# Weight-stationary projections with 256-column matmuls alone and one 256-column accumulator

## The chip, the cores and the metric

One core of a Trainium2 chip runs the whole kernel. The metric is device time in microseconds (us); a lower time is better. TensorE (PE) does the matmuls and PEld is its loading of weights, VectorE is DVE, ScalarE is ACT, GpSimd is POOL, and SyncE (SP) issues most DMAs.

## What is computed

Two residual layers over 256 positions of width 2048, each with an RMS norm ahead, and a final RMS norm. Layer 0 projects the normed input to an SSD (state-space) head group and a gated position-mixing group and projects both back; layer 1 is differential attention with 16 heads. All of it is float32.

```python
def reference(x, norm_w, even_w_in, ..., odd_w_in, ..., odd_w_out, final_norm_w):
    h = x
    for layer in range(DEPTH):
        hn = rmsnorm(h, norm_w[layer])
        i = layer // 2
        if layer % 2 == 0:
            h = h + even_mixer(hn, even_w_in[i], ...)
        else:
            h = h + odd_mixer(hn, odd_w_in[i], ...)
    return rmsnorm(h, final_norm_w)
```

In `even_mixer`, `proj = h @ w_in` is split into the SSD's gate, its x, B and C (which pass a convolution of four taps), and u, v and a gate for the position mixing; the results are concatenated and multiplied by `w_out`. In `odd_mixer`, `proj = h @ w_in` is split into q, k, v and a gate, and the attended values are multiplied by `w_out`. These four weight matrices are nearly all of the work.

## The kernel before

Every float32 operand of a large product is split into a high part in float32r and the remainder (`split` for weights, L115; `put_split` for activations, L202), and a product is the sum of three: high x high, high x low and low x high. Activations lie transposed in tiles of [128, 16, 2, 256]: 16 blocks of the contraction, the high and the low part, 256 positions.

Weights come in tiles of 128 x 2048 floats (1 MB), by one DMA each from SP's queue (`fetch`, L122). ACT writes the high part `wh` (L118) and DVE the low part `wl` (L119), in two halves of 1024 columns, with three buffers for each of `raw`, `wh` and `wl`.

Two forms of projection follow. In the weight-stationary form (`t_accum` and `t_half`, L132 to L147) a tile holds 128 output features, and PE loads a 128 x 128 block of weights and streams activations past it. It is used for B, C and x of the SSD (`conv_block`, L328), u and zb of the gating stage (L489 to L499), q and k (`qk_block`, L577) and both output projections (`out_proj`, L519). In the token-major form (`tok_proj`, L159) the activations are the stationary operand and weights stream in 512 columns; it makes z, v and the gates and is the same in both kernels.

A half tile in the weight-stationary form is 8 matmuls of 512 columns, in which `wh` meets high and low activations side by side, and then 8 of 256 columns, in which `wl` meets the high part:

```python
pe.matmul(ps, lhsT=wh[:, i, :], rhs=x[:, k, :, :].rearrange("p a b -> p (a b)"),
          start=first and k == 0, stop=False)
...
pe.matmul(ps[:, 256:512], lhsT=wl[:, i, :], rhs=x[:, k, 0, :],
          start=False, stop=last and k == 15)
```

So the accumulator `ps` (one of four PSUM banks of 512 columns, `acc`, L149) ends with high x high in its first 256 columns and the sum of the two low products in the last 256. `t_sum` (L152) joins them: ACT copies the low half to `sm` (L154), DVE adds the high half to give `t` (L156). `out_proj` does the same with L541 to L543. The one exception is the last block of the second output projection (n = 15 of "o1", L525): it already has three 256-column matmuls for each block k, in the order `wl`, `wh`, `wh`, into one accumulator (L531).

The first two tiles, B0 and C0, are handled apart at the start (L225 to L262), interleaved with the projection for dt (L245). `token_rstd` (L181) makes the norm's factor for each position: a column sum `pc_n` on PE (L187), `ms_n` on DVE, `rt_n` on POOL, a broadcast `pb_n` on PE (L194), and the copy `rb0` on ACT (L199). DVE multiplies each projection by `rb0` (L335 for the SSD, into `xp`) or `rb1` (L583).

The order of the instructions is made by a scheduler in the framework, which lists every engine's instructions by a timeline of its own; an engine then runs its list in order, and waits on semaphores.

Of the kernel before, what the change touches and what calls it, by code (L numbers as in the profile page):

```python
# [9 lines left out]
F32 = mybir.dt.float32  # L10
F32R = mybir.dt.float32r
AF = mybir.ActivationFunctionType
ALU = mybir.AluOpType
# [4 lines left out]
P = 128  # L18
S = 256
# [53 lines left out]
def hybrid_trunk(ctx: ExitStack, tc: tile.TileContext, xT, cols, dskip, dtp, lnw, lnb, sgub, wsT,  # L73
                 wdt, w0, wo0, w1, wo1, outT):
    nc = tc.nc
    v, act, pe, pool = nc.vector, nc.scalar, nc.tensor, nc.gpsimd
# [50 lines left out]
    def halves(src, inner, nm):  # L127
        raw = fetch(src, nm).rearrange("p (a b) -> p a b", b=inner)
        n = 2048 // inner // 2
        return [split(raw[:, h * n:(h + 1) * n, :], [n, inner], f"{nm}_{h}") for h in range(2)]  # L130

    def t_half(ps, hv, x, half, first, last):  # L132
        wh, wl = hv
        for i in range(8):
            k = half * 8 + i
            pe.matmul(ps, lhsT=wh[:, i, :], rhs=x[:, k, :, :].rearrange("p a b -> p (a b)"),  # L136
                      start=first and k == 0, stop=False)
        for i in range(8):
            k = half * 8 + i
            pe.matmul(ps[:, 256:512], lhsT=wl[:, i, :], rhs=x[:, k, 0, :],  # L140
                      start=False, stop=last and k == 15)

    def t_accum(ps, src, x, first, last, nm):

# [3 lines left out]

    def acc(nm):  # L149
        return acc_p.tile([P, 512], F32, tag="acc", name=f"acc_{nm}")  # L150

    def t_sum(ps, nm):  # L152
        sm = ev.tile([P, S], F32, tag="sm", name=f"sm_{nm}")
        act.activation(sm, ps[:, 256:512], AF.Copy)  # L154
        t = ev.tile([P, S], F32, tag="t", name=f"t_{nm}")
        v.tensor_tensor(t, ps[:, 0:256], sm, op=ALU.add)  # L156
        return t

    def tok_proj(srcs, x, nm):  # L159
        ps = [acc(f"{nm}_{i}") for i in range(2)]  # L160
# [48 lines left out]
    with ExitStack() as l0:  # L209
# [116 lines left out]
        def conv_block(blk, nm):  # L326
            if nm in ("B0", "C0"):
                ps = first_ps["BC".index(nm[0])]  # L328
            else:
                ps = acc(nm)  # L330
                t_accum(ps, nxt(w0), xw, True, True, nm)
            t = t_sum(ps, nm)
            xp = sp.tile([P, S + 3], F32, tag="xp", name=f"xp_{nm}", bufs=3)
            pool.memset(xp[:, 0:3], 0.0)
            v.tensor_tensor(xp[:, 3:S + 3], t, rb0, op=ALU.mult)  # L335
            cv = sp.tile([P, S], F32, tag="cv", name=f"cv_{nm}")
            act.activation(cv, xp[:, 0:S], AF.Identity, scale=c1(C_CW + blk * 4), bias=c1(C_CB + blk))
            for k in range(1, 4):
                v.scalar_tensor_tensor(cv, xp[:, k:S + k], c1(C_CW + blk * 4 + k), cv,
                                       op0=ALU.mult, op1=ALU.add)  # L340
            return cv
# [105 lines left out]
    with ExitStack() as l0b:  # L447
# [19 lines left out]
        for j in range(16):  # L467
            n = f"j{j}"
            if j % 4 == 0:
                qd = j // 4  # L470
                qs = slice(qd * 512, (qd + 1) * 512)
                lw = gp_.tile([P, 512], F32, tag="lw", name=f"lw{qd}")
                lb = gp_.tile([P, 512], F32, tag="lb", name=f"lb{qd}")
                pool.dma_start(lw, lnw[qs].rearrange("(o a) -> o a", o=1).broadcast_to([P, 512]))
                pool.dma_start(lb, lnb[qs].rearrange("(o a) -> o a", o=1).broadcast_to([P, 512]))
                with tc.issue_after(last_split[1]):
                    for tb in range(2):
                        v.tensor_scalar(vt[:, tb, qs], vt[:, tb, qs], nmu[:, tb:tb + 1], vr[:, tb:tb + 1],
                                        op0=ALU.add, op1=ALU.mult)
                    for t, op in ((lw, ALU.mult), (lb, ALU.add)):  # L480
                        v.tensor_tensor(vt[:, :, qs], vt[:, :, qs],
                                        bc(t.rearrange("p (o a) -> p o a", o=1), [P, 2, 512]), op=op)
                ws_t = gp_.tile([P, 4, P], F32, tag="ws", name=f"ws_{n}")
                pool.dma_start(ws_t, wsT[:, j:j + 4, :])
                pool.affine_select(out=ws_t, in_=ws_t, compare_op=ALU.is_ge, fill=0.0, base=0,
                                   pattern=[[0, 4], [1, P]], channel_multiplier=-1)
                sb_t = gp_.tile([P, 4, P], F32, tag="sb", name=f"sb_{n}")
                pool.dma_start(sb_t, sgub[j:j + 4, :].rearrange("(o a) b -> o a b", o=1).broadcast_to([P, 4, P]))
            ps = acc(f"u{j}")  # L489
            t_accum(ps, nxt(w0), xw, True, True, f"u{j}")  # L490
            t = t_sum(ps, f"u{j}")
            u = gp_.tile([P, S], F32, tag="u", name=f"u_{n}", bufs=3)
            v.tensor_tensor(u, t, rb0, op=ALU.mult)
            act.activation(u, u, AF.Gelu_apprx_tanh)
            ps = acc(f"zb{j}")
            t_accum(ps, nxt(w0), xw, True, True, f"zb{j}")
            t = t_sum(ps, f"zb{j}")
            zb = gp_.tile([P, S], F32, tag="zb", name=f"zb_{n}", bufs=3)
            v.tensor_tensor(zb, t, rb0, op=ALU.mult)  # L499
            act.activation(zb, zb, AF.Silu)  # L500
            pm = aux(f"pm_{n}")
            for c in range(2):
                pe.matmul(pm[:, c * P:(c + 1) * P], lhsT=vt[:, c, j * P:(j + 1) * P], rhs=ws_t[:, j % 4, :],
                          start=True, stop=True)
            mx = gp_.tile([P, 2, P], F32, tag="mx", name=f"mx_{n}")
            v.tensor_tensor(mx, pm[:, 0:S].rearrange("p (c t) -> p c t", t=P),
                            bc(sb_t[:, j % 4:j % 4 + 1, :], [P, 2, P]), op=ALU.add)
            mx = mx.rearrange("p c t -> p (c t)")
            v.tensor_tensor(mx, mx, u, op=ALU.mult)
            v.tensor_tensor(mx, mx, zb, op=ALU.mult)  # L510
            act.activation(yb[:, j, 0, :], mx, AF.Copy)
            v.tensor_tensor(yb[:, j, 1, :], mx, yb[:, j, 0, :].bitcast(F32), op=ALU.subtract)
# [6 lines left out]
    def out_proj(w, nm, after):  # L519


        pool.memset(sqa, 0.0)
        for n in range(16):
            ps = acc(f"{nm}_{n}")
            if n == 15 and nm == "o1":  # L525
                for half, x in enumerate((ya, yb)):
                    hv = halves(w[2 * n + half], P, f"{nm}_{n}{half}")
                    for k in range(16):
                        wh, wl = hv[k // 8][0][:, k % 8, :], hv[k // 8][1][:, k % 8, :]
                        for m, (lhsT, part) in enumerate(((wl, 0), (wh, 1), (wh, 0))):  # L530
                            pe.matmul(ps[:, 0:256], lhsT=lhsT, rhs=x[:, k, part, :], start=half + k + m == 0,  # L531
                                      stop=half == 1 and k == 15 and m == 2)
                v.tensor_tensor(res[:, n, :], ps[:, 0:256], res[:, n, :], op=ALU.add)
                sq = ev.tile([P, S], F32, tag="sqo", name=f"sq_{nm}_{n}")
                act.activation(sq, res[:, n, :], AF.Square)
                after(n)
                continue
            t_accum(ps, w[2 * n], ya, True, False, f"{nm}_{n}a")
            t_accum(ps, w[2 * n + 1], yb, False, True, f"{nm}_{n}b")
            sm = ev.tile([P, S], F32, tag="sm", name=f"sm_{nm}_{n}")  # L540
            act.activation(sm, ps[:, 256:512], AF.Copy)  # L541
            v.tensor_tensor(res[:, n, :], ps[:, 0:256], res[:, n, :], op=ALU.add)
            v.tensor_tensor(res[:, n, :], res[:, n, :], sm, op=ALU.add)  # L543
            sq = ev.tile([P, S], F32, tag="sqo", name=f"sq_{nm}_{n}")
            act.activation(sq, res[:, n, :], AF.Square)
            if n < 15:
                pool.tensor_tensor(sqa, sqa, sq, op=ALU.add)
            after(n)
        return [sqa, sq]
# [6 lines left out]
    with ExitStack() as l1:  # L556
# [20 lines left out]
        def qk_block(tag, c0, nm):  # L577

            ps = acc(nm)
            t_accum(ps, nxt(w1), xw, True, True, nm)  # L580
            t = t_sum(ps, nm)
            o = ap.tile([P, S], F32, tag=tag, name=nm)
            v.tensor_tensor(o, t, rb1, op=ALU.mult)  # L583
            hl = ap.tile([P, 2, S - c0], F32R, tag=tag + "hl", name=f"{nm}_hl")
            act.activation(hl[:, 0, :], o[:, c0:S], AF.Copy)
            v.tensor_tensor(hl[:, 1, :], o[:, c0:S], hl[:, 0, :].bitcast(F32), op=ALU.subtract)
            return o, hl
# [166 lines left out]
```

## Time and profile before

| | |
|---|---|
| Median of 3 runs | 1724.22 us (1722.86 to 1724.52) |
| The profiled execution: its own time | 1724.63 us |
| The profiled execution: span on the core | 1722.9 us |
| PE busy | 1702.2 us (99%), 9232 matmuls |
| PEld busy | 1460.7 us (85%) |
| DVE busy | 1126.6 us (65%) |
| ACT busy | 990.1 us (57%) |
| POOL busy | 106.0 us (6%) |
| DMA | 318.68 MB, 185 GB/s on average |

Busy time is the union of an engine's instructions. Matmuls overlap: each one's start is measured and its end is modelled, so the distance from one start to the next is what a matmul costs in a stream. In a row of the timeline the first number is the start of the first of xN instructions of one kind, and the second the time that they cover; the step within a run is the distance to the start of the next row, divided by N.

### The profile page before, as it was taken

The numbers are of one execution on the slowest core, as the hardware profiler recorded it, in microseconds if no ns is written. First come the engines' busy times: TensorE is split into PE (matmuls) and PEld (weight loads), VectorE is DVE, ScalarE is ACT, GpSimd is POOL, SyncE is SP. The second block draws the span as 40 slices with busy tenths as digits, with TensorE's granted clock in tenths as the row PEclk, the third lists the DMA queues.
The fourth block names the chain that finished last, engine by engine and source line by source line (L and its number), as shares of the span: only waits on it lengthen the run. The fifth ranks groups of instructions, "written<-read, shape, count | busy, mean of one in ns | idle before, by whom it ended". The sixth has DMA issues, their size and how long they took to land.

```text
span 1722.9 us, 23833 instructions
## 1 busy us (share of the span) xinstructions
PE 1702.2 (99%) x9232; PEld 1460.7 (85%) x9232; DVE 1126.6 (65%) x1704; ACT 990.1 (57%) x1521; POOL 106.0 (6%) x159
## 2 busy tenths in 40 slices
PE   7999999999999999999999999999999999999997
PEld 6888888888888888888888888888888888888886
DVE  6897869545777665556566666757576666655554
ACT  6776776546777744445455555555554555555443
POOL 3200000100000011110000000000000000001110
PEclk9999999999999999999999999999999999999998
DMA  7555444655655565555455455455545555445552
GB/s 254 207 175 195 172 159 171 218 198 191 216 205 173 194 236 184 193 194 172 172 188 177 171 173 191 173 173 173 184 169 184 174 180 184 171 172 196 195 191 104
DMA packets 46290, 318.68 MB, mean 185 GB/s; under 512 B 5280, under 2 KB 5584, under 8 KB 9440
## 3 DMA queue, kind: packets, MB, share of 16 engines
q1 hardware_dynamic: 44400, 310.30, 51.3%
q0 software_dynamic: 1344, 4.24, 0.9%
q10 hardware_dynamic: 432, 2.61, 0.4%
q8 instruction: 72, 1.18, 0.3%
q14 instruction: 42, 0.34, 0.1%
HBM read 315.00 MB, written 2.13 MB: 184 GB/s over the span
## 4 chain that ended last, share of the span: by engine, by line
PE 95%; DVE 1%; ACT 1%; issue 1%; POOL 1%; DMA 0%; SPq 0%; DVEq 0%; POOLq 0%; ACTq 0%
PE acc_o L136 13%; PE acc_q L136 7%; PE acc_k L136 7%; PE acc_o L140 7%; PE acc_v L170 5%; PE acc_v L172 5%; PE acc_v L171 5%; PE acc_q L140 3%; PE acc_g L172 3%; PE acc_k L140 3%; PE acc_g L170 3%; PE acc_g L171 3%; PE acc_u L136 3%; PE acc_zb L136 3%; PE acc_x L136 3%; PE acc_u L140 2%
## 5 line engine op out<-in xcount | busy, mean ns | idle before, releaser
L118 ACT ACTIVATE wh_v<-raw_v 128x1024 fp32r<-128x1024 f32 x96 | 101.8, 1060 | 109.1 <-PE acc_v L172 88.7
L119 DVE TENSOR_TENSOR wl_v<-raw_v,wh_v 128x1024 fp32r<-128x1024 f32 x96 | 117.6, 1225 | 68.3 <-ACT wh_v L118 67.4
L171 PE MATMUL acc_v<-wl_v,xw 128*128 128x512 f32 x384 | 152.2, 396 | 0.0
L172 PE MATMUL acc_v<-wh_v,xw 128*128 128x512 f32 x384 | 151.6, 395 | 0.0
L170 PE MATMUL acc_v<-wh_v,xw 128*128 128x512 f32 x384 | 142.8, 397 | 0.0
L136 PE MATMUL acc_q<-xw,wh_q 128*128 128x512 f32 x512 | 131.8, 393 | 0.0
L119 DVE TENSOR_TENSOR wl_g<-raw_g,wh_g 128x1024 fp32r<-128x1024 f32 x64 | 78.4, 1226 | 80.6 <-ACT wh_g L118 80.6
L136 PE MATMUL acc_k<-xw,wh_k 128*128 128x512 f32 x512 | 130.8, 395 | 0.0
L118 ACT ACTIVATE wh_g<-raw_g 128x1024 fp32r<-128x1024 f32 x64 | 67.9, 1060 | 80.5 <-PE acc_g L172 53.5
L119 DVE TENSOR_TENSOR wl_q<-raw_q,wh_q 128x1024 fp32r<-128x1024 f32 x64 | 77.8, 1225 | 52.0 <-ACT wh_q L118 46.5
L118 ACT ACTIVATE wh_k<-raw_k 128x1024 fp32r<-128x1024 f32 x64 | 67.8, 1059 | 70.2 <-PE acc_q L136 30.2
L118 ACT ACTIVATE wh_q<-raw_q 128x1024 fp32r<-128x1024 f32 x64 | 67.8, 1059 | 68.3 <-PE acc_g L172 23.9
L136 PEld LDWEIGHTS acc_k<-xw,wh_k 128*128 128x128 f32 x512 | 91.6, 188 | 16.2
L136 PEld LDWEIGHTS acc_q<-xw,wh_q 128*128 128x128 f32 x512 | 90.5, 188 | 15.6
L172 PE MATMUL acc_g<-wh_g,xw 128*128 128x512 f32 x256 | 101.5, 397 | 0.0
L171 PE MATMUL acc_g<-wl_g,xw 128*128 128x512 f32 x256 | 101.0, 394 | 0.0
L119 DVE TENSOR_TENSOR wl_k<-raw_k,wh_k 128x1024 fp32r<-128x1024 f32 x64 | 78.3, 1224 | 26.8 <-ACT wh_k L118 26.7
L170 PE MATMUL acc_g<-wh_g,xw 128*128 128x512 f32 x256 | 92.2, 396 | 0.0
L170 PEld LDWEIGHTS acc_v<-wh_v,xw 128*128 128x128 f32 x384 | 72.0, 187 | 16.5
L172 PEld LDWEIGHTS acc_v<-wh_v,xw 128*128 128x128 f32 x384 | 72.0, 188 | 16.3
L171 PEld LDWEIGHTS acc_v<-wl_v,xw 128*128 128x128 f32 x384 | 72.0, 188 | 16.0
L140 PE MATMUL acc_q<-xw,wl_q 128*128 128x256 f32 x512 | 73.8, 281 | 0.0
(500 smaller groups left out, 4012.6 us busy)
## 6 DMA issues: line engine op xcount, KB each, us to landing
raw_v<-in_w_dram SPq DMA_DIRECT2D x48, 1024.0 KB, 4.8
raw_q<-in_w_dram SPq DMA_DIRECT2D x32, 1024.0 KB, 4.7
raw_k<-in_w_dram SPq DMA_DIRECT2D x32, 1024.0 KB, 4.8
raw_g<-in_w_dram SPq DMA_DIRECT2D x32, 1024.0 KB, 4.8
raw_x<-in_w_dram SPq DMA_DIRECT2D x16, 1024.0 KB, 4.8
raw_z<-in_w_dram SPq DMA_DIRECT2D x16, 1024.0 KB, 4.8
raw_u<-in_w_dram SPq DMA_DIRECT2D x16, 1024.0 KB, 4.8
raw_zb<-in_w_dram SPq DMA_DIRECT2D x16, 1024.0 KB, 4.8
```

Of the source, the lines that this page charges most:

```text
L118: last_split[0] = act.activation(wh, raw, AF.Copy).ins
L119: last_split[1] = v.tensor_tensor(wl, raw, wh.bitcast(F32), op=ALU.subtract).ins
L136: pe.matmul(ps, lhsT=wh[:, i, :], rhs=x[:, k, :, :].rearrange("p a b -> p (a b)"), start=first and k == 0, stop=False)
L140: pe.matmul(ps[:, 256:512], lhsT=wl[:, i, :], rhs=x[:, k, 0, :], start=False, stop=last and k == 15)
L170: pe.matmul(ps[tb], lhsT=xh, rhs=wh, start=k == 0, stop=False)
L171: pe.matmul(ps[tb], lhsT=xh, rhs=wl, start=False, stop=False)
L172: pe.matmul(ps[tb], lhsT=xl, rhs=wh, start=False, stop=k == 15)
```

## The change

All matmuls of the weight-stationary form now have 256 columns. A half tile is three runs of eight: `wh` with the high activations, `wh` with the low ones, `wl` with the high ones. All accumulate in the first 256 columns of the bank, so there is no separate low sum: `t_sum` and its two operations for each tile are gone, DVE reads the accumulator itself, and the exception for the last block goes with them.

```diff
     def t_half(ps, hv, x, half, first, last):
         wh, wl = hv
-        for i in range(8):
-            k = half * 8 + i
-            pe.matmul(ps, lhsT=wh[:, i, :], rhs=x[:, k, :, :].rearrange("p a b -> p (a b)"),
-                      start=first and k == 0, stop=False)
-        for i in range(8):
-            k = half * 8 + i
-            pe.matmul(ps[:, 256:512], lhsT=wl[:, i, :], rhs=x[:, k, 0, :],
-                      start=False, stop=last and k == 15)
+        for m, (lhsT, part) in enumerate(((wh, 0), (wh, 1), (wl, 0))):
+            for i in range(8):
+                k = half * 8 + i
+                pe.matmul(ps[:, 0:S], lhsT=lhsT[:, i, :], rhs=x[:, k, part, :],
+                          start=first and m == 0 and k == 0, stop=last and m == 2 and k == 15)
...
-    def t_sum(ps, nm):
-        sm = ev.tile([P, S], F32, tag="sm", name=f"sm_{nm}")
-        act.activation(sm, ps[:, 256:512], AF.Copy)
-        t = ev.tile([P, S], F32, tag="t", name=f"t_{nm}")
-        v.tensor_tensor(t, ps[:, 0:256], sm, op=ALU.add)
-        return t
...
-            t = t_sum(ps, nm)
+            t = ps[:, 0:S]
...
-            if n == 15 and nm == "o1":
-                for half, x in enumerate((ya, yb)):
-                    hv = halves(w[2 * n + half], P, f"{nm}_{n}{half}")
-                    for k in range(16):
-                        wh, wl = hv[k // 8][0][:, k % 8, :], hv[k // 8][1][:, k % 8, :]
-                        for m, (lhsT, part) in enumerate(((wl, 0), (wh, 1), (wh, 0))):
-                            pe.matmul(ps[:, 0:256], lhsT=lhsT, rhs=x[:, k, part, :], start=half + k + m == 0,
-                                      stop=half == 1 and k == 15 and m == 2)
...
             t_accum(ps, w[2 * n], ya, True, False, f"{nm}_{n}a")
             t_accum(ps, w[2 * n + 1], yb, False, True, f"{nm}_{n}b")
-            sm = ev.tile([P, S], F32, tag="sm", name=f"sm_{nm}_{n}")
-            act.activation(sm, ps[:, 256:512], AF.Copy)
-            v.tensor_tensor(res[:, n, :], ps[:, 0:256], res[:, n, :], op=ALU.add)
-            v.tensor_tensor(res[:, n, :], res[:, n, :], sm, op=ALU.add)
+            v.tensor_tensor(res[:, n, :], ps[:, 0:S], res[:, n, :], op=ALU.add)
```

The line `t = t_sum(...)` is replaced in the same way for u, zb, q and k.

The scheduler lists the new program anew. The two places that follow are on PE. At the first, near the start, x_1 is the fourth SSD block and `acc_B` with the larger number is the fifth, the one that takes the bank of B0. Before:

```order
L140 MATMUL acc_x_1_428<-xw,wl_x_1_1_436 128x256 [waits DVE_49]
L140 MATMUL acc_x_1_428<-xw,wl_x_1_1_436 128x256 x7
L136 MATMUL acc_B_547<-xw,wh_B_0_550 128x512 [waits Activation_49]
L136 MATMUL acc_B_547<-xw,wh_B_0_550 128x512 x7
L140 MATMUL acc_B_547<-xw,wl_B_0_551 128x256 [waits DVE_49]
L140 MATMUL acc_B_547<-xw,wl_B_0_551 128x256 x5
L194 MATMUL pb_n_272<-ident,rt_n_270 128x128 [waits Pool_49]
```

The same place on PE in the changed kernel:

```order
L137 MATMUL acc_x_1_464<-xw,wl_x_1_1_472 128x256 [waits DVE_49]
L137 MATMUL acc_x_1_464<-xw,wl_x_1_1_472 128x256
L184 MATMUL pb_n_304<-ident,rt_n_302 128x128 [waits Pool_49]
L184 MATMUL pb_n_304<-ident,rt_n_302 128x128
L264 MATMUL pz<-ident,dt_zT 128x32 x2
L137 MATMUL acc_x_1_464<-xw,wl_x_1_1_472 128x256 x6
L137 MATMUL acc_B_595<-xw,wh_B_0_598 128x256 [waits DVE_49]
```

The broadcast `pb_n` moved ahead of the block B, and this block's first matmul waits for DVE where it waited for ACT. On DVE in the changed kernel, the products that free the banks of B0 and C0 (`xp`, which read the accumulators) stand behind the small operations on dt:

```order
L119 TENSOR_TENSOR wl_B_1_603<-raw_B_596,wh_B_1_602 128x1024 [waits PE_49,Activation_49]
L273 SCALAR_TENSOR_TENSOR dt_z<-pz,rt_n_302,dtv 128x32 [waits DMASW1_49,PE_49,Pool_49]
L273 SCALAR_TENSOR_TENSOR dt_z<-pz,rt_n_302,dtv 128x32
L275 SCALAR_TENSOR_TENSOR dt_e<-dt_z 128x64 [waits DVE_49]
L325 TENSOR_TENSOR xp_B_376<-acc_B_187,rb_n_307 128x256 [waits Activation_49]
L325 TENSOR_TENSOR xp_C_385<-acc_C_188,rb_n_307 128x256
```

Before, `xp` read the tile `t` in SBUF, and a weight split stood between `dt_z` and `xp`.

The second place on PE is the passage from the gating stage (its last mixing product `pm`) to the first output projection. Before:

```order
L503 MATMUL pm_j_5671<-ws_j_5239,vt 128x128 x2
L136 MATMUL acc_o_0_5689<-ya,wh_o_0a_5692 128x512 x8
L140 MATMUL acc_o_0_5689<-ya,wl_o_0a_5693 128x256 x8
L136 MATMUL acc_o_0_5689<-ya,wh_o_0a_5696 128x512 x8
L140 MATMUL acc_o_0_5689<-ya,wl_o_0a_5697 128x256 x8
```

The same place in the changed kernel:

```order
L493 MATMUL pm_j_6439<-ws_j_5911,vt 128x128 x2
L137 MATMUL acc_o_0_6457<-ya,wh_o_0a_6460 128x256 x16
L137 MATMUL acc_o_0_6457<-ya,wl_o_0a_6461 128x256 x8
L137 MATMUL acc_o_0_6457<-ya,wh_o_0a_6464 128x256 x16
L137 MATMUL acc_o_0_6457<-ya,wl_o_0a_6465 128x256 x8
```

From here on 1,536 matmuls of 256 columns follow each other with nothing between them, where runs of 512 and of 256 columns alternated. In the gating stage a pair of `pm` products stands after every 96 of them.

## Rows read from the trace of the kernel before

**Rows 1.** The page's head: busy time by engine, and the granted clock in 40 slices.

```profile
PE 1702.2 (99%) x9232; PEld 1460.7 (85%) x9232; DVE 1126.6 (65%) x1704; ACT 990.1 (57%) x1521; POOL 106.0 (6%) x159
...
PEclk9999999999999999999999999999999999999998
```

**Rows 2.** The three longest waits of PE: us in total, times, longest.

```profile
PE acc_dt L245 <- DVE wd L241: 8.0, 1, 8.0
PE pda L305 <- POOL xp_x L334: 1.3, 1, 1.3
PE pb_n L194 <- POOL rt_n L191: 1.0, 1, 1.0
```

**Rows 3.** One window in the last output projection: busy us and instructions, PEclk, DMA.

```profile
1588.00:1698.30 110.30, 110.30 (x641) 97.13 (x641) 56.65 (x61) 53.30 (x70) 14.39 (x10) 1.00 0.52 182
```

**Rows 4.** Timeline of PE, two tiles' end: start, us covered, count.

```profile
1691.21 2.00 PE L136 MATMUL acc_o<-ya,wh_o_14a 128*128 128x512 f32 x8
1693.05 1.07 PE L140 MATMUL acc_o<-ya,wl_o_14a 128*128 128x256 f32 x8
1693.95 1.99 PE L136 MATMUL acc_o<-yb,wh_o_14b 128*128 128x512 f32 x8
1695.78 1.11 PE L140 MATMUL acc_o<-yb,wl_o_14b 128*128 128x256 f32 x8
1696.72 2.00 PE L136 MATMUL acc_o<-yb,wh_o_14b 128*128 128x512 f32 x8
```

**Rows 5.** Timeline of PE: first of the last block's 96 matmuls, what follows them.

```profile
1699.46 0.28 PE L531 MATMUL acc_o<-ya,wl_o 128*128 128x256 f32 x1
...
1710.35 0.50 PE L187 MATMUL pc_n<-ones,sqa 128*128 128x1 f32 x4
```

**Rows 6.** Timeline of PE in the attention stage.

```profile
804.14 2.00 PE L136 MATMUL acc_q<-xw,wh_q 128*128 128x512 f32 x8
805.98 1.10 PE L140 MATMUL acc_q<-xw,wl_q 128*128 128x256 f32 x8
806.92 2.00 PE L136 MATMUL acc_k<-xw,wh_k 128*128 128x512 f32 x8
808.76 1.11 PE L140 MATMUL acc_k<-xw,wl_k 128*128 128x256 f32 x8
809.71 2.00 PE L136 MATMUL acc_k<-xw,wh_k 128*128 128x512 f32 x8
...
814.41 0.38 PE L624 MATMUL pt_h<-ident,at_h 128*128 128x128 f32 x2
814.55 1.19 PE L140 MATMUL acc_k<-xw,wl_k 128*128 128x256 f32 x8
815.58 2.00 PE L136 MATMUL acc_k<-xw,wh_k 128*128 128x512 f32 x8
```

**Rows 7.** Line 140's matmuls by tile: duration ns, least/median/most.

```profile
L140 PE MATMUL acc_q<-xw,wl_q x512: 276/279/363, 773.2 to 1473.0; 128*128 128x256 f32 x171
L140 PE MATMUL acc_k<-xw,wl_k x512: 276/279/364, 785.4 to 1484.5; 128*128 128x256 f32 x171
```

**Rows 8.** Groups of the low sum: count, busy us, mean ns, idle before.

```profile
L154 ACT ACTIVATE sm_q<-acc_q 128x256 f32<-128x256 f32 x32 | 12.0, 375 | 0.4
...
L156 DVE TENSOR_TENSOR t_q<-acc_q,sm_q 128x256 f32<-128x256 f32 x32 | 13.3, 417 | 0.0
```

**Rows 9.** Timeline near the start: `pb_n` on PE, `rb0` on ACT, DVE up to `xp`.

```profile
41.58 0.60 PE L194 MATMUL pb_n<-ident,rt_n 128*128 128x128 f32 x4
...
42.35 0.50 PE L140 MATMUL acc_B<-xw,wl_B 128*128 128x256 f32 x2
...
42.22 0.38 ACT L199 ACTIVATE rb_n<-pb_n 128x256 f32<-128x256 f32 x1
...
42.96 1.23 DVE L119 TENSOR_TENSOR wl_C<-raw_C,wh_C 128x1024 fp32r<-128x1024 f32 x1
44.10 0.42 DVE L335 TENSOR_TENSOR xp_B<-t_B,rb_n 128x256 f32<-128x256 f32 x1
```

More of the change, by code (lines that the diff above doesn't have):

```diff
@@ L490, in hybrid_trunk @@
             t_accum(ps, nxt(w0), xw, True, True, f"u{j}")
-            t = t_sum(ps, f"u{j}")
+            t = ps[:, 0:S]
             u = gp_.tile([P, S], F32, tag="u", name=f"u_{n}", bufs=3)
@@ L496, in hybrid_trunk @@
             t_accum(ps, nxt(w0), xw, True, True, f"zb{j}")
-            t = t_sum(ps, f"zb{j}")
+            t = ps[:, 0:S]
             zb = gp_.tile([P, S], F32, tag="zb", name=f"zb_{n}", bufs=3)
@@ L524, in out_proj @@
             ps = acc(f"{nm}_{n}")
-            if n == 15 and nm == "o1":
-                for half, x in enumerate((ya, yb)):
-                    hv = halves(w[2 * n + half], P, f"{nm}_{n}{half}")
-                    for k in range(16):
-                        wh, wl = hv[k // 8][0][:, k % 8, :], hv[k // 8][1][:, k % 8, :]
-                        for m, (lhsT, part) in enumerate(((wl, 0), (wh, 1), (wh, 0))):
-                            pe.matmul(ps[:, 0:256], lhsT=lhsT, rhs=x[:, k, part, :], start=half + k + m == 0,
-                                      stop=half == 1 and k == 15 and m == 2)
-                v.tensor_tensor(res[:, n, :], ps[:, 0:256], res[:, n, :], op=ALU.add)
[L534 to L537, printed above, removed]
             t_accum(ps, w[2 * n], ya, True, False, f"{nm}_{n}a")
             t_accum(ps, w[2 * n + 1], yb, False, True, f"{nm}_{n}b")
-            sm = ev.tile([P, S], F32, tag="sm", name=f"sm_{nm}_{n}")
-            act.activation(sm, ps[:, 256:512], AF.Copy)
-            v.tensor_tensor(res[:, n, :], ps[:, 0:256], res[:, n, :], op=ALU.add)
-            v.tensor_tensor(res[:, n, :], res[:, n, :], sm, op=ALU.add)
+            v.tensor_tensor(res[:, n, :], ps[:, 0:S], res[:, n, :], op=ALU.add)
             sq = ev.tile([P, S], F32, tag="sqo", name=f"sq_{nm}_{n}")
@@ L580, in qk_block @@
             t_accum(ps, nxt(w1), xw, True, True, nm)
-            t = t_sum(ps, nm)
+            t = ps[:, 0:S]
             o = ap.tile([P, S], F32, tag=tag, name=nm)
```

## The prediction, made before the changed kernel had run

> **What bounds the kernel now.** The page's first table comes first: PE has matmuls in flight for 1702.2 of 1722.9 us, and the granted clock stays at the upper of its two levels, 2.4 GHz, all through [rows 1]. Then the chain of waits on PE: 8.0 us before the first matmul, and after that single waits of 1.3 us and less, none of them for the low sum's copy or addition [rows 2]. So time is the sum of PE's steps from one matmul's start to the next one's start, and the next views are there to price a step. (The matmuls' durations overlap each other, since their ends are modelled; only starts are used for prices.)
>
> In a stretch of the last output projection that holds nothing but 40 half tiles, 110.30 us passed, 2.757 us for a half tile of 8 wide and 8 narrow matmuls [rows 3]. The timeline there shows both kinds [rows 4]: eight 512-column matmuls take 1.83 to 1.84 us (229 ns a step). Eight 256-column ones take 0.90 us in one half tile and 0.94 us in the next: the narrow matmul has **two steps, a short one of 113 ns and a long one of 117.7 ns**, and a whole half tile takes 2.74 or 2.77 us accordingly. In the same rows weights, moving data and accumulator are of the same shape, so the step belongs to how a run was entered, and a run keeps it. The last block of the second projection is already written with 256 columns alone: from 1699.46 to 1710.35 us, 96 matmuls, 113.4 ns each, with no change within the run [rows 5]. It began behind a run with the short step. In the attention stage the long step is the common one, as from 805.98 to 806.92 and from 808.76 to 809.71. And the run behind the transposes, 814.55 to 815.58, takes 1.03 us for eight: its first step is wider still, and what is left, about 0.83 us for seven, is the long step again [rows 6]. The durations say how common it is: the short step goes with 276 ns (the least), the long one with 279 to 280, and the median is 279 over the 512 low matmuls of q and over the 512 of k [rows 7]. So more than half have the long step.
>
> **The change, part by part.** There are 384 half tiles: 64 tiles in layer 0, 64 in layer 1, 64 in the two projections, two halves each. Four of them (the last block) have the new form already, so 380 change.
>
> 1. *Matmuls.* Per half tile, 8 wide and 8 narrow become 24 narrow; the columns streamed stay 768, the weight loads go from 16 to 24. Now: 2.757 us where the two steps alternate (124 half tiles of the projections) [rows 3], about 2.775 where the long step is the more common (256 others; 2.78 and 2.79 for those that start at 804.14 and 806.92) [rows 6]; the weighted mean is 2.77. Then, at the long step: 24 x 117.7 ns = 2.825 us, 0.055 more, times 380 = **+21 us**. At the short step: 24 x 113.4 = 2.722 us, 0.048 less, times 380 = **-18 us**. Sign and size hang on which step it is, and break-even is at 2.77 / 24 = 115.4 ns, where a little over half of the matmuls have the short one. I take the long step. The wide matmul, from whose stream a run can come out at either step, is gone between the runs; the order shows the new runs entered from transposes and other small full-precision matmuls, 96 long in the gating stage and nearly 1,500 long in each projection, and the entry from transposes that the trace shows led to the long step [rows 6]. The uncertain point is that the trace has nothing beyond eight matmuls in a row at the long step, and 96 at the short one [rows 5].
>
> The Trainium skill has a rule against this change: by "TensorE: Matmul & The Clock Gate", section "Back-to-back issue gap", a matmul costs its columns at 2.4 GHz and about 2.5 ns, so that two of 256 columns cost 2.5 ns more than one of 512. By that rule the sum would be 8 x 2.5 ns x 380, an estimate of +8 us. The trace does not agree: a wide step is 229 ns, and two narrow ones are 227 or 235 [rows 4, 5].
>
> 2. *The last block* had 96 matmuls at 113.4 ns [rows 5]. They now sit at the end of a long run and share its step: 96 x 4.3 ns = +0.4 us at the long one. The steps behind them (addition, square, norm) stay.
>
> 3. *The low sum.* ACT loses 128 copies of about 0.37 us in `t_sum` and 31 in `out_proj`, DVE as many additions of 0.42 us [rows 8]. That is some 58 and 66 us of engine time beside PE, which waits for neither [rows 2]: 0 us. If this cover were gone, all of it could count, but PE is covered at 99% [rows 1]. For the same reason transfers that start earlier gain nothing.
>
> 4. *A new wait at the start.* Without the sum, accumulators B0 and C0 come free only when DVE has multiplied them by `rb0`. The second B block takes B0's bank, and its first matmul, which waited for ACT alone, now waits for DVE, with the whole PE queue behind it. The order has put the norm's broadcast `pb_n` ahead of this block. Counted from the start of `pb_n` (41.58 before): the copy of `rb0` on ACT ended 1.02 us later [rows 9]; with two small DVE operations and the product of 0.42 us, the bank is free after about 1.5 to 2.0 us. PE has `pb_n` and `pz` until 0.77 us and then six narrow matmuls, so it arrives after 1.5 us. It costs 0 if `rb0` is early; if DVE puts a split of 1.23 us in between, as it did before [rows 9], 1.5 us. I take 0.5, since the new DVE order has no split there.
>
> Sum: 1724.63 (the profiled execution, 0.4 above the median of the three runs) + 21 + 0.4 + 0.5 = 1746.5; less 0.5 for the few runs that come out of the token-major projections at the short step, **1746 us**.
>
> **The rivals.** *The short step everywhere (faster).* If the step of those 96 matmuls is where every run ends up, all drop to 113.4 ns: 1724.6 - 18 + 0.5 = 1707 us. For it: the longest run in the trace has it from end to end. Against it: that run was entered from one that had it, and the entry from transposes gives the other. It decides from the point where somewhat more than half of the 9,216 matmuls have the short step. Chance 0.15.
>
> *The short step in the long runs alone.* The two projections (124 half tiles) settle at 2.722, 124 x (2.722 - 2.757) = -4 us; the shorter runs elsewhere keep the long step, 256 x (2.825 - 2.775) = +13 us. With the wait that gives 1734 us. Chance 0.12. A single fixed cost for every matmul, as the skill's rule has it, would land close by, at 1733 by its estimate.
>
> *A longer wait, or an order that starves PE.* The program is ordered anew, with accumulators that DVE alone frees. It adds 2 to 8 us to the forecast if several such waits appear, 1748 to 1754 us. Against it: four accumulators, and DVE loses work. Chance 0.03.
>
> **How the numbers follow.** Forecast 0.70, the others as given. A change of up to 0.2% (3.4 us) is about what a measurement of this kernel cannot tell from none. The forecast's own range is 1739 (2.775 now throughout, a fifth of the matmuls at the short step) to 1753 (2.757 now throughout, a wait of 1.5). The range reaches down into the mixed case: 1726 to 1753, which leaves out the faster case and little else. Slower is the forecast, the longer wait and nearly all of the mixed case, 0.80; faster 0.16; same 0.04.
>
> **What would show it.** In the profile after: eight narrow matmuls in 0.94 us throughout both projections, a median duration of 279 for them, 113 us for 40 half tiles in place of 110.30 [rows 3], and no wait on PE over 2 us beyond the first. Runs at 0.90 us with durations of 276 would make it wrong, as would a mixture with more than half of them so.

## The result and the profile after

The changed kernel takes 1751.67 us (median of 4 runs, 1751.38 to 1751.93), the kernel before 1723.54 beside it (4 runs, 1722.11 to 1724.52): a ratio of 1.0165, 95% interval 1.0152 to 1.0178. The forecast was 1746 with a range of 1726 to 1753. The profiled executions differ by 27.3 us, 1750.2 against 1722.9 us of span.

First the head of the page of the changed kernel, which answers to [rows 1]:

```profile
PE 1724.8 (99%) x12272; PEld 1611.9 (92%) x12272; DVE 1064.8 (61%) x1545; ACT 950.2 (54%) x1358; POOL 98.7 (6%) x159
...
PEclk9999999999999999999999999999999999999999
```

PE is still the bound, and has 22.6 us more of busy time. DVE and ACT lost 62 and 40 us, and the time did not follow them. Weight loads, 9232 before, are now 12272, 92% of the span.

Then the stretch of 40 half tiles in the last output projection, and two short stretches at the start (window, us, busy us and instructions of PE, PEld, DVE, ACT and POOL, then the granted clock as PEclk, DMA share, GB/s), against [rows 3]:

```profile
1590.81:1703.88 113.07, 113.07 (x962) 113.07 (x961) 52.38 (x50) 51.74 (x61) 10.77 (x10) 1.00 0.53 187
56.00:60.00 4.00, 1.75 (x14) 1.74 (x15) 2.54 (x6) 1.86 (x3) 2.03 (x6) 0.96 0.53 217
60.00:63.00 3.00, 3.00 (x16) 2.94 (x14) 2.11 (x4) 0.15 (x1) 0.10 (x1) 0.50 0.25 55
```

The 40 half tiles take 113.07 us instead of 110.30: 2.827 us each, or 117.8 ns for each of 24 narrow matmuls. The timeline of PE in that stretch (start, us covered, count) shows it for every group: 8 narrow matmuls start 0.94 us apart from the next group, 16 of them 1.89.

```profile
1700.11 1.10 PE L137 MATMUL acc_o<-yb,wl_o_12b 128*128 128x256 f32 x8
1701.05 2.05 PE L137 MATMUL acc_o<-yb,wh_o_12b 128*128 128x256 f32 x16
1702.94 1.10 PE L137 MATMUL acc_o<-yb,wl_o_12b 128*128 128x256 f32 x8
1703.88 2.05 PE L137 MATMUL acc_o<-ya,wh_o_13a 128*128 128x256 f32 x16
```

The durations by tile (ns, least/median/most), which answer to [rows 7], stand at 279 as before:

```profile
L137 PE MATMUL acc_q<-xw,wl_q x512: 276/279/365, 790.4 to 1495.9; 128*128 128x256 f32 x171
...
L137 PE MATMUL acc_k<-xw,wl_k x512: 276/279/281, 802.8 to 1507.5; 128*128 128x256 f32 x171
```

Read from start to start, 8624 of the steps between neighbouring narrow matmuls lie at 116 to 121 ns and only 319 at 112 to 115. The 1,536 matmuls of projection 0, in one run from 607.05 us on, have the long step from end to end. Of the runs of any length three alone came out at the short one, from 23.28, 42.91 and 825.52 us on, of 97, 112 and 91 matmuls. The step changes nowhere but where a wait or other work on PE interrupts a run.

Where the time went, by the first matmul of each stage on PE (us from the span's start; the third and fourth kernels are experiments below):

| first matmul of | before | changed | sum operations kept | hybrid |
|---|---|---|---|---|
| v (end of the SSD stage) | 319.6 | 328.6 | 323.4 | 320.1 |
| projection 0 | 594.3 | 607.0 | 602.0 | 592.8 |
| q | 771.2 | 788.4 | 783.4 | 767.4 |
| (last one of projection 1) | 1710.2 | 1737.7 | 1733.1 | 1704.3 |

From v on it is 18.5 us (27.5 at the last matmul less 9.0 at v), with 0.4 for the last block and 57 ns for each of 316 changed half tiles. Up to v it is 9.0 us, and 64 half tiles at 50 to 57 ns are only 3.2 to 3.6 of these. The rest belongs to the start. The waits of PE there (total us, times, longest), against [rows 2]:

```profile
PE acc_dt L235 <- DVE wd L231: 8.0, 1, 8.0
PE pda L295 <- POOL xp_x L324: 2.4, 1, 2.4
PE pc_n L177 <- POOL xp_C L324: 2.3, 1, 2.3
PE pb_n L184 <- POOL rt_n L181: 1.0, 1, 1.0
...
PE acc_B L137 <- DVE xp_B L325: 0.2, 1, 0.2
```

The wait of 2.3 us for `pc_n`, the column sum of the first norm, is new, and that for `pda` is 1.1 us longer. The wait that the prediction had named, the second B block for the product that frees B0's bank, is the last line: 0.2 us. The timeline of POOL and of PE shows what `pc_n` waits for. POOL was named for a small memset, but its addition of line 250 ran for 6.53 us; `sqs`, which `pc_n` reads, was ready at 37.0.

```profile
29.68 6.53 POOL L250 TENSOR_TENSOR sq<-sq 128x512 f32<-128x512 f32 x1
36.29 0.73 POOL L251 TENSOR_TENSOR sqs<-sq 128x256 f32<-128x256 f32 x1
...
37.07 0.61 PE L177 MATMUL pc_n<-ones,sqs 128*128 128x1 f32 x4 [2.28 <-POOL xp_C L324]
...
58.25 0.40 PE L295 MATMUL pda<-ident,dt_z 128*32 128x128 f32 x2 [2.37 <-POOL xp_x L324]
58.40 1.19 PE L137 MATMUL acc_x<-xw,wl_x 128*128 128x256 f32 x8
59.43 3.39 PE L137 MATMUL acc_x<-xw,wh_x 128*128 128x256 f32 x16
```

In the kernel before, the same two additions took 2.50 and 1.61 us:

```profile
29.23 2.50 POOL L260 TENSOR_TENSOR sq<-sq 128x512 f32<-128x512 f32 x1
31.81 1.61 POOL L261 TENSOR_TENSOR sqs<-sq 128x256 f32<-128x256 f32 x1
```

Behind the wait for `pda` time is lost a second time. In the window from 56 to 60 us PE was busy for 1.75 of 4 us, and from 60 to 63 us the granted clock is 0.50 of full speed, 1.2 GHz: the 16 narrow matmuls from 59.43 take 3.18 us to the next start (62.61), where 16 in the projection take 1.89. Behind the wait for `pc_n`, which was nearly as long, the clock stayed at 1.00:

```profile
37.00:41.00 4.00, 3.93 (x33) 3.93 (x34) 1.54 (x3) 1.18 (x2) 1.03 (x7) 1.00 0.31 123
```

### The profile page after: what moved, and what is told of

Its sections match the earlier page's. It is cut to its first block, busy times and chain, and to the rows that moved or that the text cites. A ratio compares the mean times of both kernels' runs of the same rounds, so it can differ in the third digit from the quotient of the medians.

```text
span 1750.2 us, 29646 instructions
## 1 busy us (share of the span) xinstructions
PE 1724.8 (99%) x12272; PEld 1611.9 (92%) x12272; DVE 1064.8 (61%) x1545; ACT 950.2 (54%) x1358; POOL 98.7 (6%) x159
## 4 chain that ended last, share of the span: by engine, by line
PE 95%; POOL 2%; ACT 1%; issue 1%; DVE 1%; DMA 1%; SPq 0%; DVEq 0%; POOLq 0%; ACTq 0%
PE acc_o L137 20%; PE acc_q L137 10%; PE acc_k L137 10%; PE acc_zb L137 5%; PE acc_u L137 5%; PE acc_v L162 5%; PE acc_v L161 5%; PE acc_v L160 5%; PE acc_x L137 5%; PE acc_g L162 3%; PE acc_g L160 3%; PE acc_g L161 3%; PE acc_C L137 2%; PE acc_B L137 2%; PE acc_z L161 2%; PE acc_z L160 2%
## 5 line engine op out<-in xcount | busy, mean ns | idle before, releaser
L137 PE MATMUL acc_q<-xw,wh_q 128*128 128x256 f32 x1024 | 134.0, 280 | 0.0
L137 PE MATMUL acc_k<-xw,wh_k 128*128 128x256 f32 x1024 | 133.4, 280 | 0.0
L137 PEld LDWEIGHTS acc_q<-xw,wh_q 128*128 128x128 f32 x1024 | 126.8, 188 | 0.6
L137 PEld LDWEIGHTS acc_k<-xw,wh_k 128*128 128x128 f32 x1024 | 125.9, 188 | 0.0
```

Source lines behind the costliest of these rows:

```text
L137: pe.matmul(ps[:, 0:S], lhsT=lhsT[:, i, :], rhs=x[:, k, part, :], start=first and m == 0 and k == 0, stop=last and m == 2 and k == 15)
```

## The experiments

The theory (A): a narrow matmul with new weights has two steps, and what stands ahead of a run settles which one the run keeps. The rival (B): a stream that loads weights for every 256 columns costs 118 ns, whatever comes before it. For the start: the wait behind `rb0` that the prediction named, against the later norm.

**Wide matmuls thrown in (`kicks`).** In both projections, from the third tile on, one to four additional 512-column matmuls into a spare bank stand in the first run of each half tile, 112 groups.

```diff
+    if kick[0] is not None and m == 0 and i == 2 + at:
+        for _ in range(wides):
+            pe.matmul(kick[0], lhsT=wh[:, i, :], rhs=x[:, k, :, :]..., start=True, stop=True)
```

> The changed kernel, with 112 short groups of one to four 512-column matmuls put into both output projections, each into a spare bank that nothing reads, behind the third to fifth of the first eight narrow matmuls of a half tile; 24 narrow matmuls lie between two groups. Theory A (the step belongs to how a run was entered): after a group whose last wide matmul has a duration of 394 ns the narrow matmuls run at 113.4 ns up to the next group, after any other at 117.7; both steps appear in one stage, with the same weights, tiles and banks. Theory B (the step belongs to the place, the accumulator or the weights' address): 117.7 ns after every group. Time, with 280 wide matmuls of 229 ns: 1751.7 + 64 = about 1816 us by B, about 1811 by A if four groups in ten end at the short step.

Measured: 1812.6 us (one execution). The timeline of PE, with a group of two, of three, of four and of one:

```profile
642.05 0.63 PE L146 MATMUL spare_o<-ya,wh_o_3a 128*128 128x512 f32 x2
642.51 1.46 PE L142 MATMUL acc_o<-ya,wh_o_3a 128*128 128x256 f32 x11
643.81 1.10 PE L142 MATMUL acc_o<-ya,wl_o_3a 128*128 128x256 f32 x8
...
645.11 0.86 PE L146 MATMUL spare_o<-ya,wh_o_3a 128*128 128x512 f32 x3
645.81 1.64 PE L142 MATMUL acc_o<-ya,wh_o_3a 128*128 128x256 f32 x13
647.28 1.07 PE L142 MATMUL acc_o<-ya,wl_o_3a 128*128 128x256 f32 x8
...
648.64 1.07 PE L146 MATMUL spare_o<-yb,wh_o_3b 128*128 128x512 f32 x4
...
650.97 1.10 PE L142 MATMUL acc_o<-yb,wl_o_3b 128*128 128x256 f32 x8
...
652.50 0.40 PE L146 MATMUL spare_o<-yb,wh_o_3b 128*128 128x512 f32 x1
...
654.03 1.10 PE L142 MATMUL acc_o<-yb,wl_o_3b 128*128 128x256 f32 x8
```

Behind three wide matmuls eight narrow ones cover 1.07 us (0.91 to the next start), behind one, two or four they cover 1.10 (0.94). That held for all 28 groups of each size, until the next group. (The groups of four stand behind the short stream that three had left, the others behind a long one.) So theory A holds in that what stands ahead decides, and the step is not drawn by chance. The sign that the expectation gave for the outcome, a duration of 394 ns of the group's last wide matmul, does not hold: groups of two end with 394 ns as well and left all 28 runs at the long step. The time agrees: 280 wide steps of 229 ns are 64.1 us, 28 stretches of about 24 narrow steps at 4.4 ns less are -3.0, and 1751.7 + 64.1 - 3.0 is 1812.8.

**The bank freed early (`free_first`).** In the first four blocks ACT copies the accumulator, so that the bank need not wait for `rb0`.

```diff
+            if nm in ("B0", "C0", "x0_0", "x0_1"):
+                t = ev.tile([P, S], F32, tag="t", name=f"t_{nm}")
+                act.activation(t, ps[:, 0:S], AF.Copy)
```

> The changed kernel, with the first four accumulators (B0, C0 and the two x blocks) copied by ACT to SBUF, so that their banks come free without the norm's factor, as before the change. If the extra 6 us of the start come from the banks: about 1746 us, and no wait of the second B block for xp. If they come from the column sum of the norm, which the new order places 2.3 us too early: about 1751 us, with the same 2.3 us of wait on PE.

Measured: 1749.55 us (1749.06 to 1750.24), ratio to before 1.0149 (1.0134 to 1.0164). The wait for `xp_B` is gone, those for `pc_n` and `pda` are down to 1.4 and 1.3 us, and v starts at 326.7. The addition on POOL still takes 5.42 us. That is neither of the two cases expected: the wait for `xp_B` went, but the time stayed 3.5 us above 1746 us, and the wait for `pc_n` did not stay at 2.3 us. The stretch at 1.2 GHz did not go away; it came earlier, behind the shorter wait for `pc_n`:

```profile
36.29 0.61 PE L177 MATMUL pc_n<-ones,sqs 128*128 128x1 f32 x4 [1.35 <-POOL xp_C L327]
...
38.37 3.24 PE L137 MATMUL acc_x<-xw,wh_x 128*128 128x256 f32 x16
...
38.00:41.00 3.00, 3.00 (x16) 3.00 (x16) 1.23 (x1) 0.34 (x1) 0.00 (x0) 0.50 0.08 11
```

**POOL relieved (`short_pool`).** PE sums four parts of the squares; POOL's last two additions are left out.

```diff
-            pool.tensor_tensor(sq[:, 0, 0:2], sq[:, 0, 0:2], sq[:, 0, 2:4], op=ALU.add)
-            pool.tensor_tensor(sqs, sq[:, 0, 0, :], sq[:, 0, 1, :], op=ALU.add)
-            rt0, rb0 = token_rstd([sqs], "n0")
+            rt0, rb0 = token_rstd([sq[:, 0, i, :] for i in range(4)], "n0")
```

> The changed kernel, with the last two of POOL's five additions for the norm's column sum left out; PE sums the four remaining columns of squares instead, by 6 more pairs of one-column matmuls. POOL spends 7.2 us less ahead of the column sum. If the waits at the start are POOL's lateness: the 2.3 us wait for the column sum and most of the 2.4 us wait for the transposed step sizes go, and so does the stretch at half the clock that follows them; about 1747 us. If the 28 us are the matmuls' step alone: 1751 to 1753 us.

Measured: 1749.05 us (1748.47 to 1749.83), ratio 1.0146 (1.0131 to 1.0161). `pc_n` no longer waits at the start, `pda` waits 1.4 us, no stretch there has the lower clock, and v starts at 324.9, 3.7 us earlier than in the changed kernel. The time lies between the 1747 us expected if POOL's lateness is the cause and the 1751 us if it plays no part, so POOL's additions account for a large part of the loss at the start and not for all of it.

**The sum's operations kept (`keep_sum_ops`).** The matmuls of the changed kernel, but ACT's copy and an operation of DVE between the accumulator and the product stay in `conv_block`, the u and zb tiles and `qk_block` (they take the larger of two equal values, so they add nothing).

```diff
+        act.activation(sm, ps[:, 0:S], AF.Copy)
+        v.tensor_tensor(t, ps[:, 0:S], sm, op=ALU.max)
```

> The changed kernel, with ACT's copy and DVE's second operation kept for each of the 128 tiles of B, C, x, u, zb, q and k: ACT copies the accumulator, DVE takes the maximum of the two equal values and writes it to SBUF. If the low sum's removal is worth nothing, as predicted: within 2 us of the changed kernel, less what the banks' earlier release gives at the start (0 to 6 us). If ACT and DVE were close to holding PE up in the new form, the removal paid for part of the loss: slower than 1755 us.

Measured: 1747.93 us (1747.08 to 1748.05), ratio 1.0140 (1.0123 to 1.0156): 3.7 us less than without them. POOL's addition is back at its old duration,

```profile
29.75 2.50 POOL L257 TENSOR_TENSOR sq<-sq 128x512 f32<-128x512 f32 x1
32.33 1.60 POOL L258 TENSOR_TENSOR sqs<-sq 128x256 f32<-128x256 f32 x1
```

and among the waits `pc_n` at the start has none, `pda` 1.1 us. v starts at 323.4 us, so of the 9.0 us that were lost up to there, 5.2 go with these operations and their order, and 3.8 are left, about what 64 half tiles at 50 to 57 ns account for. From v to the last matmul this kernel takes 1409.7 us, the changed one 1409.1. So away from the start the low sum of the u, zb, q and k tiles is worth nothing. (That of `out_proj` was not put back here.)

**Real wide matmuls at each tile's head (`three_wide`, `two_wide`).** For the first three (two) blocks of a tile the two narrow matmuls of the high weights become one wide one, and the sum is kept. The columns streamed stay the same.

```diff
+        for i in range(wide):
+            pe.matmul(ps, lhsT=wh[:, i, :], rhs=x[:, half * 8 + i, :, :]..., start=first and i == 0, stop=False)
         for m, (lhsT, part) in enumerate(((wh, 0), (wh, 1), (wl, 0))):
-            for i in range(8):
+            for i in range(wide if m < 2 else 0, 8):
```

> Each tile with stationary weights (but for B0, C0 and the last block) begins with three 512-column matmuls for its first three blocks; these blocks' two narrow matmuls are left out, and the low half is summed on ACT and DVE as in the kernel before. The columns streamed are those of the changed kernel; per tile 6 narrow steps become 3 wide ones. Theory A (the entry decides a run's step): three wide matmuls in a row are the dose that brought 28 of 28 runs of the experiment with added wide matmuls to 113 ns, so most tiles come to 113 ns and the projections and the attention stage lose 45 narrow steps x 4.4 ns = 0.2 us a tile; about 125 of 158 tiles short gives some -25 us against 1749, so 1715 to 1730. If the dose depends on where in its cycle the stream before it stands, and tiles with three wide ones return to the long step, the time stays at 1744 to 1752. Theory B (weight loads alone set the step): all narrow matmuls stay at 118 ns, 1747 to 1751.

> The same with two 512-column matmuls at the head of each tile. Theory A: in the experiment with added wide matmuls two of them left or put every run at the long step (28 of 28), so 1745 to 1752 and narrow steps at 118 ns, except where the stream before stands at another point of its cycle. Theory B: 1747 to 1751, 118 ns throughout.

Measured: 1743.97 us (1743.06 to 1744.90, ratio 1.0118, 1.0101 to 1.0135) and 1738.72 (one execution). With three, 18% of the narrow steps are short; with two, 32%. Neither did what the group's size alone had promised (1715 to 1730 us with three, 1745 to 1752 with two). In the trace the outcome goes with the durations of the wide matmuls, which are read here as a sign of where in a cycle the stream before stood. From a stream at the long step they mostly begin in one of three ways, 392, 394 ns or 397, 394, 394 or 397, 397, 392, and the tile comes out short after the second, after the third, or not yet; seven tiles with three wide matmuls began 392, 388, 392 and stayed long. From a stream at the short step 25 of 29 go 388, 392, 394, and three leave these short; the other four begin with 394 and come out long. Two make all 17 long. In projection 0 with two at each head, the 14 tiles from the third on alternate, short and long, to the last.

**The dose by place (`dosed`).** So the number of wide matmuls at a tile's head, its dose, was set by what these two traces showed for each entry: 4 at the head of projection 0, of the third tile of projection 1, of most u tiles and of a few others, 2 in the q and k tiles whose wide matmuls had begun with 392 and 394, else 3.

```diff
+        if nm in DOSE:
+            return DOSE[nm]
+        return 4 if nm[0] == "u" and int(nm[1:]) > 2 else 3
+    DOSE = {"o0_0a": 4, "o1_2a": 4, "zb0": 2, "C2": 4, ..., "k0_00": 2}
```

> As the kernel with three wide matmuls at each tile's head, with their number set by what the two kernels before showed for the entry of each tile: 4 instead of 3 at the head of projection 0, at its counterpart (third tile) in projection 1, and in the u tiles from the fourth on; 2 in one zb tile, in the second q tile and the third k tile of each head; 3 elsewhere. Theory A: a stream whose wide matmuls end on the right point of the cycle goes on at 113.4 ns, and from a stream at 113.4 ns three wide ones keep it there; both projections (15 and 14 tiles of 96 narrow steps) then stand at 113.4 ns and lose some 12 us, the gating stage 5 us and the attention stage 3 us: about 1724, between 1718 and 1732. If a projection's later tiles fall back to 117.8 ns in spite of the dose, 1736 to 1744. Theory B (weight loads alone): unchanged at 1744.

Measured: 1724.73 us (10 runs, 1722.49 to 1729.55), ratio 1.0009 (1.0000 to 1.0019), 76% of the narrow steps short. At the head of projection 0 in the kernel with three wide matmuls everywhere:

```profile
602.05 0.94 PE L135 MATMUL acc_o<-ya,wh_o_0a 128*128 128x512 f32 x3
602.83 1.34 PE L140 MATMUL acc_o<-ya,wh_o_0a 128*128 128x256 f32 x10
604.01 1.10 PE L140 MATMUL acc_o<-ya,wl_o_0a 128*128 128x256 f32 x8
```

and in the dosed kernel, whose stream then keeps the short step through the whole projection:

```profile
596.44 1.18 PE L135 MATMUL acc_o<-ya,wh_o_0a 128*128 128x512 f32 x4
597.46 1.07 PE L140 MATMUL acc_o<-ya,wh_o_0a 128*128 128x256 f32 x8
598.36 1.07 PE L140 MATMUL acc_o<-ya,wl_o_0a 128*128 128x256 f32 x8
...
769.82 1.07 PE L140 MATMUL acc_o<-yb,wl_o_15b 128*128 128x256 f32 x8
```

**Doses corrected (`dosed2`), and with POOL relieved (`dosed2_pool`).** Eight places where the dosed kernel's trace had shown the wrong number (five of them go back to 3); the second also has the edit of `short_pool`.

```diff
+    DOSE = {..., "B4": 4, "B6": 4, "k0_00": 4}
+    DOSE["q0_01"] = 3
```

> The dosed kernel with the doses that its trace showed to be off corrected: four wide matmuls instead of three at the head of two B tiles and of the first k tile, three instead of four in the last k tile of three heads, three instead of two in zb0. Theory A: these tiles and their followers come to 113.4 ns, about 9 tiles x 0.19 us, 1.5 to 2 us less than the dosed kernel: 1721 to 1724, on the side of the kernel before or 0.1% ahead of it. Theory B: as the dosed kernel, 1724 to 1725.

> The same with the column sum of the first norm's squares done by PE on four parts instead of by POOL's two additions, as in the experiment with the short POOL work. That took 2.6 us off the changed kernel; if the wait for POOL is worth the same here, 1718.5 to 1722; if another wait takes its place, as that of the kernel before, no difference, 1721 to 1724.

Measured: 1722.18 us (11 runs, 1721.83 to 1723.07), ratio 0.9995 (0.9986 to 1.0004), and 1723.20 (11 runs, 1721.87 to 1726.17), ratio 1.0000 (0.9991 to 1.0010). The doses are worth less than the 2.5 us between the two medians: the intervals of `dosed` and `dosed2` overlap, and in the traces the last matmul starts at 1707.7 us instead of 1708.6, 0.9 us earlier, about what 180 more short steps at 4.4 ns give. Relieving POOL showed no gain here. In its profiled execution, one of the slower ones at 1725.72 us, the wait for `pda` rose from 1.7 to 2.8 us and a stretch at 1.2 GHz stands behind it.

**The old form up to v, doses behind it (`hybrid`).** All B, C and x tiles go back to eight wide and eight low matmuls; the rest is as in `dosed2`.

```diff
+        if nm[0] in "BCx":
+            return 8
```

> The B, C and x tiles of layer 0 (and so the whole start) in the form of the kernel before, with eight wide and eight low matmuls; the u, zb, projection and attention tiles dosed as in the last kernels. If the 4 us by which all kernels of the new form reach the first token-major tile later than the kernel before come from the start and the SSD stage alone, they are gone: first v tile at 319.6 us instead of 323, total 1718 to 1720, ratio to before 0.997 to 0.9985. If the step of the first u tiles comes out long and is not mended by four wide matmuls, 1722 to 1726.

Measured: 1717.86 us (5 runs, 1716.16 to 1718.84), ratio 0.9962 (0.9948 to 0.9975). This kernel is faster than both, by 0.4% than the kernel before, and a little below the 1718 to 1720 us expected. v starts at 320.1 us (323.5 in `dosed2`), from there to the last matmul it takes the 1384.2 us of `dosed2`, and the stretch of 40 half tiles in the last projection takes 108.86 us, against 110.30 [rows 3] and 113.07 (each of its tiles has three wide matmuls at its head):

```profile
1573.83:1682.69 108.86, 108.86 (x933) 107.63 (x931) 56.60 (x60) 53.31 (x71) 14.11 (x10) 1.00 0.57 194
```

## Why the prediction was right, and where it was off

*The matmuls* (step 1) were the forecast's main term, and it held. 2.825 us for a half tile at the long step was predicted, 2.827 measured. With the last block +21.4 us was predicted, and 18.5 us from v on with the 3.8 us left up to v in `keep_sum_ops`, 22.3 us, measured. From v on the step's own figures give 124 x (2.825 - 2.757) + 192 x (2.825 - 2.775) + 0.4 = 18.4 us, against 18.5. The uncertain point was decided as forecast: entered from transposes and other small full-precision matmuls, the runs took the long step, but for the one from 825.52 us on (of the other two short ones, one came from the 512-column matmuls of dt, one from the wait for `xp_B`), and a run kept it over 1,536 matmuls. That the entry decides, which the prediction had argued from [rows 4 to 6], is now shown, by 112 added groups and by the dosed kernel, where four wide matmuls at the head of projection 0 in place of three moved the step of its 16 tiles.

*The rivals.* The short step everywhere and the short step in the long runs alone did not come about. The first one's price of a half tile was right, since the hybrid shows half tiles at 2.722 us; the entries that lead there were missing.

*The last block* (step 2): its 96 matmuls took the step of the long run that they end, as predicted.

*The low sum* (step 3) was priced at nothing beside PE. Away from the start that is right to 0.6 us, for the tiles whose operations were put back. At the start it is wrong in sign: taking the operations out cost 5.2 us of span, in which the norm came later behind POOL's long addition; `short_pool`, without that addition, got 3.7 us of it back.

*The new wait at the start* (step 4) is the term that was mis-sized: 0.5 us, bounds 0 to 1.5, against 5.2. The wait that it named exists and took 0.25 us. Of the signs that the prediction named, one failed here: there was to be no wait on PE over 2 us beyond the first, and there were two. What was not seen is that the first norm's column sum, which PE must do before anything can be scaled, waits for POOL. In the rows: 2.28 us before `pc_n`, 1.1 more before `pda`, 0.25 before the B block, and 1.3 us more for 16 matmuls in the stretch at 1.2 GHz, 4.9 in all. The rival "an order that starves PE" had the right kind and a chance of 0.03; here it came on top of the forecast, and the measured time lies in its 1748 to 1754. Without these 5.2 us the changed kernel would have been at 1751.7 - 5.2 = 1746.5, beside the forecast of 1746. That 1751.7 still lies in the range is in part luck: the end at 1753 was made of a price before of 2.757 us for every half tile and a wait of 1.5 us, and neither was so. (The forecast's own lower end, 1739, comes out nearer 1737 with the 2.775 us that it names; nothing hangs on it.) The 0.5 us taken off for runs that come out of the token-major projections short was wrong in kind: those runs were long, and the three short ones stood behind others.

Why POOL's addition needs 6.53 us in one kernel and 2.50 in another was not isolated. It is 2.50 in the three kernels that have the sum of the first two tiles on DVE (before, `keep_sum_ops`, `hybrid`) and 5.4 to 6.5 in all seven others that have the addition, so that what DVE does beside it is the likely cause. The rows of DVE fit that. Before, the sum `t_B` stands ahead of a weight split, POOL's addition ends at 31.73 us within this split, and the split takes 1.65 us instead of 1.21:

```profile
30.83 0.40 DVE L156 TENSOR_TENSOR t_B<-acc_B,sm_B 128x256 f32<-128x256 f32 x1
31.16 1.65 DVE L119 TENSOR_TENSOR wl_x<-raw_x,wh_x 128x1024 fp32r<-128x1024 f32 x1
```

In the changed kernel four splits and two sums for dt follow one another on DVE without a gap from 29.81 us on, and POOL's addition ends at 36.21, 1.1 us behind the last of them:

```profile
33.88 1.21 DVE L119 TENSOR_TENSOR wl_B<-raw_B,wh_B 128x1024 fp32r<-128x1024 f32 x1
```

That is argued, not shown. Open too are what inside PE makes the two steps, and why the clock fell behind some of the waits at the start and not behind others.

## What to carry to other kernels

Before matmuls are split to smaller ones for the sake of other engines, look in the trace for the step from start to start of the small form, and for whether it has more than one value; the average of a mixture says little about a stream made of one kind alone. If a stream keeps the step with which it was entered, the entry is worth tuning, and a few instructions at its head can be worth more than the form of the other hundreds. Where work is taken off an engine with slack, look at the stretches where that engine and its neighbours feed PE first, at the program's start above all, since the slack of the whole says nothing about those.

## What the runs showed that was not expected

- 256-column matmuls with new weights for each have steps of 113.3 and 117.8 ns. A run held the long one for 1,536 matmuls in a row, and the short one through the 16 tiles of projection 0 in `dosed`, three or four wide matmuls at each head included. Added 512-column matmuls moved the step with the same outcome in 28 of 28 groups of each of four sizes, which always came in the same order.
- The number of wide matmuls alone does not decide: at the tiles' heads the outcome went with their modelled durations, which mostly show one of three beginnings on a stream at the long step (392 then 394, 397 then 394, or 397 twice), and so how many more are needed.
- An addition of 128 x 512 on POOL took 2.50 or 6.53 us in kernels that differ only in what the other engines do beside it.
- Behind a wait of 2.37 us on PE the granted clock was 0.50 from 60 to 63 us, and in `free_first` behind one of 1.35 us it was 0.50 from 38 to 41 us; behind a wait of 2.28 us in the changed kernel it stayed at 1.00 from 37 to 41 us. The length of the wait alone does not decide it.
